# RMSNorm with swish on one Trainium2 core: the last two units of eight rows are swished separately instead of together

## The chip, the cores and the metric

The kernel runs on one core of a Trainium2 chip. The metric is device time in microseconds (us), as the median of several runs. A profile of one execution comes with each kernel: its span is the stretch that the hardware profiler covers, and the execution's own time is somewhat longer than the span.

Four engines work on the data of this kernel or wait for it: VectorE (DVE in the profile), ScalarE (ACT), GpSimd (POOL) and SyncE (SP, which issues all transfers). TensorE (PE) computes nothing here; its queue is used to merge waits.

## The reference

The input x has 16 x 1024 rows of 512 float32 values, gamma has 512 values. Each row is divided by its root mean square, scaled by gamma, and swished (the value times its sigmoid):

```python
def reference(x: np.ndarray, gamma: np.ndarray, eps: float) -> np.ndarray:
    rms = np.sqrt(np.mean(x ** 2, axis=-1, keepdims=True) + eps)
    x_norm = x / rms * gamma
    return (x_norm * (1.0 / (1.0 + np.exp(-x_norm)))).astype(np.float32)
```

So 33.55 MB are read from the chip's memory and 33.55 MB are written to it.

## The kernel before

**Tiling.** The 16384 rows are spread over 128 partitions, 128 rows in each. Rows are counted per partition below, so "row 96" is one row of 512 values in each of the 128 partitions. The rows are worked in units of eight (`cn = 8`), so there are 16 units (`K = 16`), number 0 to 15. On chip they lie in one buffer `xb`, a ring of 96 rows, where everything is done in place: the load writes a unit there, VectorE scales it there, ScalarE swishes it there, and the store reads it from there. Rows 96 to 127 take the places of rows 0 to 31.

**Transfers.** They are larger than a unit, and SyncE issues them all, in an order written out by hand (`order`, L33 to L37), through one hardware queue that 16 DMA engines serve. A piece is a first row and a number of rows. The stores are

```python
    stores = [(0, 32), (32, 32), (64, 16), (80, 16), (96, 24), (120, 8)]
```

A store waits, on SyncE, until the counter `s_swish` has reached the number of units that it needs (`ends`, L56; the wait is at L121 and L122). For the store of rows 96 to 119 that is 15 units, for the one of rows 120 to 127 it is 16. Since SyncE works its list in order, a store that waits holds what comes behind it on SyncE. The last loads are issued after the store of rows 0 to 31 has landed, and before the other stores. At the very end SyncE waits for all stores (L170).

**The work on a unit.** ScalarE squares six of its rows and adds them up (`square`, L211 to L221; L215 is the operation), VectorE does the same for the other two (`sums`, L243 to L250). GpSimd adds eps and raises to the power -0.5 (L183, L189). VectorE multiplies each of the eight rows by its factor and by gamma, one instruction for a row (`norm`, L252 to L259; L255 is the operation), and adds 1 to the counter `s_norm` after the last. ScalarE takes that from `s_norm` and swishes the unit in one instruction (`swish`, L223 to L225), and adds to `s_swish`.

**The order on the engines.** ScalarE's loop (L233 to L240) squares the unit two ahead and then swishes the unit at hand; it runs for units 0 to 13. After the loop, units 14 and 15 are left to swish, and there is nothing left to square. They lie side by side in the ring, and L241 swishes them in one instruction of 16 rows, after a wait for both. VectorE's loop (L267 to L279) sums the next unit and scales the unit at hand, for units 0 to 14; L281 scales unit 15. `take` waits for a number on a counter and lowers the counter by it:

```python
    def take(queue, sem, n=1):
        queue.wait_ge(sem, n).then_inc(sem, -n)
```

Of the kernel before, what the change touches and what calls it, by code (L numbers as in the profile page):

```python
# [9 lines left out]
def kernel(  # L10
# [7 lines left out]
    nc = tc.nc  # L18
    P = nc.NUM_PARTITIONS
    AF = mybir.ActivationFunctionType  # L20
# [18 lines left out]
    cn = 8  # L39
# [13 lines left out]
    K = rows_each // cn  # L53
# [37 lines left out]
    s_norm = nc.alloc_semaphore("s_norm")  # L91
    s_swish = nc.alloc_semaphore("s_swish")
# [4 lines left out]
    def take(queue, sem, n=1):  # L97
        queue.wait_ge(sem, n).then_inc(sem, -n)  # L98
# [9 lines left out]
    def buf(piece):  # L108
        a, n = piece
        at = a % ring  # L110
        assert at + n <= ring, piece
        return xb[:, at : at + n, :]
# [40 lines left out]
    for what, a in order[early:]:  # L153
# [4 lines left out]
        elif what == "gamma":  # L158
            need(
                nc.sync.dma_start(  # L160
                    out=gamma4[0:P:32, :], in_=gamma.partition_broadcast(4)
# [19 lines left out]
    for k in range(K):  # L181
        need(
            nc.gpsimd.tensor_scalar(  # L183
                out=aeps[k % 2], in0=ms[min(k, 1)], scalar1=eps_f, scalar2=None, op0=ALU.add,
# [5 lines left out]
                out=rstd[:, k * cn : (k + 1) * cn], in0=aeps[k % 2], in1=neg_half, op=ALU.pow  # L190
# [13 lines left out]
    def row_of(unit, r, n=1):  # L204
        return flat[:, r * D : ring * D - size + (r + n) * D][:, bass.ds(unit, n * D)]
# [14 lines left out]
        done[-1].then_inc(s_acc, 1)  # L220
        return done  # L221

    def swish(rows, n=1):  # L223
        take(nc.scalar, s_norm, n)
        nc.scalar.activation(out=rows, in_=rows, func=AF.Silu).then_inc(s_swish, n)  # L225

    nc.scalar.preload_act_table_set("silu_and_others")  # L227
    take(nc.scalar, s_land)
# [4 lines left out]
    with nc.scalar.Fori(0, (K - 2) * size, size) as i:  # L233
        new, old = unit_of(i + 2 * size), unit_of(i)
        sq_rows = [row_of(new, r) for r in range(cn - own)]
        old_rows = row_of(old, 0, cn)
        addresses(nc.scalar, [old_rows] + sq_rows)
        take(nc.scalar, s_land)
        square(ms[1], junk, sq_rows)
        swish(old_rows)  # L240
    swish(buf(((K - 2) * cn, 2 * cn)), 2)  # L241

    def sums(to, rows):  # L243
        n = len(rows)
# [22 lines left out]
    with nc.vector.Fori(0, (K - 1) * size, size) as i:  # L267
        new, old = unit_of(i + size), unit_of(i)
        rows = [row_of(old, r) for r in range(cn)]
# [10 lines left out]
    k = K - 1  # L280
# [39 lines left out]
```

## Time and profile before

| | |
|---|---|
| median of 3 runs | 161.79 us (161.56 to 162.26) |
| the profiled execution's own time | 161.8 us |
| its span | 160.5 us |
| VectorE busy | 107.6 us (67%) |
| ScalarE busy | 115.5 us (72%) |
| GpSimd busy | 42.9 us (27%) |
| the DMA queue's packets, share of 16 engines' span | 97.7% |
| memory read and written | 67.12 MB, mean 418 GB/s over the span |
| swishes of eight rows (L225), 14 | mean 3605 ns |
| swish of sixteen rows (L225), 1 | 7030 ns |
| VectorE's scaling of one row (L255), 128 | mean 746 ns |

How to read it: a line such as L225 is a line of the kernel's file, and since `swish` is a helper, all swishes have that line. Busy time counts operations on data, not waits or the issuing of transfers. Scalings follow each other in a pipeline, so eight in a row take less than eight times the mean of one. An issue of a transfer stands under SyncE (SPq) and takes little; the transfer itself lands later, and its packets show only in the views of the DMA. In these, a packet is counted whole in the window in which it starts.

### The profile page before, as it was taken

The numbers are of one execution on the slowest core, as the hardware profiler recorded it, in microseconds if no ns is written. First come the engines' busy times: TensorE is split into PE (matmuls) and PEld (weight loads), VectorE is DVE, ScalarE is ACT, GpSimd is POOL, SyncE is SP. The second block draws the span as 40 slices with busy tenths as digits, with TensorE's granted clock in tenths as the row PEclk, the third lists the DMA queues.
The fourth block names the chain that finished last, engine by engine and source line by source line (L and its number), as shares of the span: only waits on it lengthen the run. The fifth ranks groups of instructions, "written<-read, shape, count | busy, mean of one in ns | idle before, by whom it ended". The sixth has DMA issues, their size and how long they took to land. (4 is left out here: it accounts for less than half of the span.)

```text
span 160.5 us, 847 instructions
## 1 busy us (share of the span) xinstructions
DVE 107.6 (67%) x198; ACT 115.5 (72%) x204; POOL 42.9 (27%) x38
## 2 busy tenths in 40 slices
DVE  0043999798988989898909898989899990000000
ACT  3159389999999999999189999999998009700000
POOL 1004506052441606153305160614325000000000
DMA  7999999999999997969999999969979999299997
GB/s 265 445 427 433 433 482 392 441 474 392 427 397 483 523 441 343 523 270 498 408 392 474 391 419 546 490 294 523 474 310 417 474 408 417 114 588 392 392 392 327
DMA packets 2744, 67.12 MB, mean 418 GB/s; under 512 B 308, under 2 KB 308, under 8 KB 312
## 3 DMA queue, kind: packets, MB, share of 16 engines
q1 hardware_dynamic: 2744, 67.12, 97.7%
HBM read 33.56 MB, written 33.55 MB: 418 GB/s over the span
## 5 line engine op out<-in xcount | busy, mean ns | idle before, releaser
L255 DVE SCALAR_TENSOR_TENSOR xb<-xb,rstd,gamma_sb 128x512 f32 (+1 forms) x128 | 86.1, 746 | 0.0
L225 ACT ACTIVATE xb<-xb (+1 forms) x15 | 57.5, 3834 | 9.4 <-ACTq L98 9.4
L215 ACT ACTIVATE junk<-xb 128x512 f32 (+1 forms) x94 | 54.7, 582 | 12.8 <-ACTq L98 12.8
L246 DVE SCALAR_TENSOR_TENSOR junk_v<-xb 128x512 f32 (+1 forms) x34 | 22.1, 689 | 24.8 <-DVEq L98 24.8
L189 POOL TENSOR_TENSOR rstd<-aeps,neg_half 128x8 f32<-128x8 f32 x16 | 31.8, 1985 | 1.3
L183 POOL TENSOR_SCALAR aeps<-ms 128x8 f32<-128x8 f32 x16 | 10.3, 647 | 78.8 <-DVE junk_v L246 78.8
L215 ACT ACTIVATION_READ_ACCUMULATOR junk<-xb 128x1 f32 x94 | 17.8, 189 | 0.0
L246 DVE DVE_READ_ACCUMULATOR junk_v<-xb 128x1 f32 x34 | 2.8, 83 | 0.0
L227 ACT ACT_TABLE_LOAD x1 | 1.3, 1283 | 1.9 <-PEq L62 1.9
L178 POOL MEMSET gamma<- 128x512 f32 x1 | 0.5, 525 | 1.5 <-POOLq L62 1.5
L263 DVE STREAM_SHUFFLE gamma_sb<-gamma 128x512 f32<-128x512 f32 x1 | 0.7, 718 | 0.0
L301 POOL MEMSET const-float32-0.0<- 128x1 f32 x1 | 0.1, 98 | 0.2 <-issue 0.2
L179 POOL MEMSET neg_half<- 128x8 f32 x1 | 0.1, 105 | 0.0
L301 POOL MEMSET const-bfloat16-1.0<- 128x1 bf16 x1 | 0.1, 102 | 0.0
L301 POOL MEMSET const-uint8-127<- 128x1 uint8 x1 | 0.1, 101 | 0.0
L301 POOL MEMSET const-float32-1.0<- 128x1 f32 x1 | 0.1, 98 | 0.0
L263 DVE LOAD_MASK_SELECT gamma_sb<-gamma x1 | 0.0, 13 | 0.0
## 6 DMA issues: line engine op xcount, KB each, us to landing
xb<-in_x_dram SPq DMA_DIRECT2D x4, 4096.0 KB, 29.7
out_dram<-xb SPq DMA_DIRECT2D x2, 4096.0 KB, 31.0
xb<-in_x_dram SPq DMA_DIRECT2D x3, 2048.0 KB, 13.8
out_dram<-xb SPq DMA_DIRECT2D x1, 6144.0 KB, 15.9
xb<-in_x_dram SPq DMA_DIRECT2D x1, 2816.0 KB, 43.0
xb<-in_x_dram SPq DMA_DIRECT2D x1, 2560.0 KB, 25.0
xb<-in_x_dram SPq DMA_DIRECT2D x2, 1024.0 KB, 5.7
out_dram<-xb SPq DMA_DIRECT2D x1, 2048.0 KB, 20.4
```

Of the source, the lines that this page charges most:

```text
L178: nc.gpsimd.memset(gamma4, 0.0).then_inc(s_zero, 1)
L179: nc.gpsimd.memset(neg_half, -0.5).then_inc(s_half, 1)
L183: nc.gpsimd.tensor_scalar(out=aeps[k % 2], in0=ms[min(k, 1)], scalar1=eps_f, scalar2=None, op0=ALU.add,),
L189: nc.gpsimd.tensor_tensor(out=rstd[:, k * cn : (k + 1) * cn], in0=aeps[k % 2], in1=neg_half, op=ALU.pow),
L215: nc.scalar.activation(out=dummies[j], in_=rows[j], func=AF.Square, scale=inv_d**0.5, accum_out=sums[:, j : j + 1],)
L225: nc.scalar.activation(out=rows, in_=rows, func=AF.Silu).then_inc(s_swish, n)
L227: nc.scalar.preload_act_table_set("silu_and_others")
L246: ins = nc.vector.scalar_tensor_tensor(out=junk_v[j], in0=rows[j], scalar=inv_d, in1=rows[j], op0=ALU.mult, op1=ALU.mult, accum_out=to[:, ...
L255: ins = nc.vector.scalar_tensor_tensor(out=rows[j], in0=rows[j], scalar=factors[j], in1=gamma_sb, op0=ALU.mult, op1=ALU.mult,)
L263: need(nc.vector.stream_shuffle(gamma_sb, gamma4, [0] * 32), s_gld, 16).then_inc(s_gamma, 1)
L301: nc = _bacc.Bacc("TRN2", target_bir_lowering=False, num_devices=1)
```

## The change

`swish` loses its parameter for a number of units, and takes one from `s_norm` and adds one to `s_swish`. Where units 14 and 15 were swished by one instruction of 16 rows, a loop issues two instructions of eight rows, each after a wait for its own unit. The loads, the stores, their order and the other engines' instructions are as before.

```diff
@@ -220,9 +220,9 @@
-    def swish(rows, n=1):
-        take(nc.scalar, s_norm, n)
-        nc.scalar.activation(out=rows, in_=rows, func=AF.Silu).then_inc(s_swish, n)
+    def swish(rows):
+        take(nc.scalar, s_norm)
+        nc.scalar.activation(out=rows, in_=rows, func=AF.Silu).then_inc(s_swish, 1)
@@ -238,7 +238,8 @@
         take(nc.scalar, s_land)
         square(ms[1], junk, sq_rows)
         swish(old_rows)
-    swish(buf(((K - 2) * cn, 2 * cn)), 2)
+    for k in range(K - 2, K):
+        swish(buf((k * cn, cn)))
```

Lines behind L241 move down by one in the changed file.

## The prediction

> **What bounds the kernel now.** I read the chain of waits first, because it shows where the last engine instruction ended, then SyncE's own waits, then the 40 slices, and last the DMA share in short windows of the tail, because only those show transfers.
>
> The chain that ended last, in order of time (start, length, what):
>
> ```profile
> 132.49 0.07 issue
> 132.56 7.03 ACT xb L225
> ```
>
> It stops at 132.56 + 7.03 = 139.59 us, although the span is 160.5 us. The chain knows engine instructions only; the 20.9 us after it belong to transfers. SyncE's own waits (line, what ended the wait, total us, times, longest):
>
> ```profile
> SPq L121 <- ACT xb L225: 42.0, 2, 29.7
> SPq L170 <- DMA out_dram<-xb: 20.0, 1, 20.0
> ```
>
> The reader sees a store (L121) held for 29.7 us by a swish (L225), and then SyncE with nothing left but to wait 20.0 us for stores. Which store: the list of issues from 139 us on has exactly two, of 6144 and 2048 KB, which are rows 96 to 119 and 120 to 127; 288 packets, 8.39 MB in all:
>
> ```profile
> q1 hardware_dynamic: 288, 8.39, 88.9%
> ...
> out_dram<-xb SPq DMA_DIRECT2D x1, 6144.0 KB, 15.9
> out_dram<-xb SPq DMA_DIRECT2D x1, 2048.0 KB, 20.4
> ```
>
> Now the engines before that, in order of time (start, length, engine, line), ScalarE and then VectorE:
>
> ```profile
> 120.27 3.60 ACT L225 ACTIVATE xb<-xb  x1
> 132.56 7.03 ACT L225 ACTIVATE xb<-xb 128x8192 f32<-128x8192 f32 x1 [8.69 <-ACTq L98]
> ```
>
> ```profile
> 121.75 10.69 DVE L255 SCALAR_TENSOR_TENSOR xb<-xb,rstd,gamma_sb 128x512 f32 x16
> ```
>
> ScalarE idles 8.69 us while VectorE scales both last units, eight rows each, in one unbroken stretch; the first unit is done halfway, and nothing takes it up. Last, the transfers in short windows (DMA share is the mean over 16 engines, the last column GB/s; a packet is counted whole in the window where it starts, so a short window can show more than 1):
>
> ```profile
> core 0: us, DVE busy (x) ACT busy (x) POOL busy (x), PEclk, DMA share, GB/s
> 100.00:131.00 31.00, 29.30 (x52) 23.87 (x40) 10.72 (x8) 1.00 0.97 421
> 131.00:137.00 6.00, 1.43 (x3) 4.44 (x1) 0.00 (x0) 1.00 1.01 437
> 137.29:137.32 0.03, 0.00 (x0) 0.03 (x1) 0.00 (x0) 1.00 2.54 1092
> 137.32:140.44 3.12, 0.00 (x0) 2.27 (x1) 0.00 (x0) 1.00 0.00 0
> 140.44:140.60 0.16, 0.00 (x0) 0.00 (x0) 0.00 (x0) 1.00 11.70 4915
> 153.20:153.37 0.17, 0.00 (x0) 0.00 (x0) 0.00 (x0) 1.00 10.71 4626
> 155.02:155.20 0.18, 0.00 (x0) 0.00 (x0) 0.00 (x0) 1.00 3.47 1457
> 159.30:159.47 0.17, 0.00 (x0) 0.00 (x0) 0.00 (x0) 1.00 3.62 1542
> 159.47:160.47 1.00, 0.00 (x0) 0.00 (x0) 0.00 (x0) 1.00 0.01 0
> ```
>
> Share times window times 16 is packet time. At 137.29 that is 2.54 x 0.03 x 16 = 1.22 us: one packet, the last of the older stores, so its engine is free at 137.31 + 1.22 = 138.53. At 140.44 it is 30.0 us: all 16 engines start the 6144 KB store, at 1.87 us a packet. Transfers fill the core's DMA engines up to 137 us (421 and 437 GB/s), then nothing starts for 3.12 us, then the last 8.39 MB run. So DMA bounds the kernel, with one hole, and the hole ends by the 16-row swish.
>
> **The change part by part.** The sum is made against the profiled execution: span 160.47, time 161.8, so 1.33 lie outside; 161.8 is 0.01 above the median of 161.79, so I carry the result over as it is.
>
> 1. Swish of unit 14 alone. VectorE ends that unit at 121.75 + 10.69/2 = 127.10. ScalarE starts some 0.12 later (VectorE's end at 132.44 to ScalarE's start at 132.56), at 127.22, and takes 3.60 (the eight-row row above): done at 130.82, not 139.59. This is the value that the store of rows 96 to 119 waits for (15 units). From the swish's end to the first packets took 140.44 - 139.59 = 0.85 in the tail of before, so its packets are ready at about 131.7. No engine is free before about 137.56: the window 136.34 to 137.32 shows a share of 1.24, that is 1.24 x 0.98 x 16 / 1.215 = 16 packets, the last one of each engine, and they end from 137.56 to 138.53. Slack 5.9 us.
>
> 2. Swish of unit 15. VectorE still ends at 132.44; ScalarE, free since 130.82, runs 132.56 to 136.16, and the 2048 KB store is ready at about 137.0. It is wanted only after eight packets per engine of the store ahead, some 14.6 us later. What the split adds on ScalarE, 2 x 3.60 - 7.03 = 0.17, and one more wait and semaphore step, lie in that cover; without it they would cost 0.17 plus about 0.1.
>
> 3. New overlap: from 127.22 to 130.82 ScalarE swishes beside VectorE's scaling. In the loop eight such scalings took 5.39 beside ScalarE's work, here 10.69/2 = 5.35: 0.04 later for unit 15, covered as in 2. A gain of as much is excluded, since VectorE waits for nothing there.
>
> 4. SyncE. No issue is added or moved in order: the wait for 15 units ends near 130.8 in place of 139.6, the 2048 KB store now waits some 5.3 us for unit 15, and only the final wait (L170) is behind it. An issue takes 0.35. POOL's last work ended at 124.7; nothing of it is passed. The loads are long landed, so nothing collides with an earlier store.
>
> 5. The DMA hole. With packets ready at 131.7, each engine goes from its last older packet straight into the new store. What a hand-over costs I take from the hand-over between the last two stores: at 153.20 to 153.37 all engines start their last packet of 10.71 x 0.17 x 16 / 16 = 1.82 us, so they end at 155.02 to 155.19, and in 155.02 to 155.20 all 16 start the next store. Cost 0, to 0.01. The other bound is what a store pays with nothing ahead: 0.85 to start, and 160.47 - 160.09 = 0.38 from the last byte (159.47 + 0.62) to the end, 1.23 together. I take 0: it is the same kind of transition. Below 0 is excluded, an engine's packets follow in order.
>
> 6. The tail itself. Per engine 8 x 1.82 + 8 x 0.616 (3.62 x 0.17 x 16 / 16) = 19.49. Check: 88.9% of the 22 us queried is 19.56, which holds the first packet's 0.05 extra.
>
> The end is set by the last engine, since a store is dealt out to engines in fixed parts: 138.53 + 19.49 + 0.38 = **158.40**, against 160.47: 2.07 less. Time 161.8 - 2.1 = **159.7** (-1.3%). The hole looks like 3.1 us in the windows, but an engine still works 1.22 us after its last start; that is why I don't take 3.1.
>
> Against this stands a statement of the Trainium skill, "DMA: Bandwidth & Descriptors", section "Anatomy of one DMA": each transfer carries a fixed cost of about 2.0 us besides its bytes, most of it the receipt of the last write. If the queue paid that at a hand-over, the estimate would be 2.07 - 2.0, no gain. The row at 155.02 disagrees that a queued store pays it (0.01 us); what the trace shows at the very end is 0.38 us.
>
> **The rivals.**
>
> A, above: 159.7.
>
> B, the engines even out. At the hole the older stores end spread from 137.56 to 138.53; if the last engine stood at the middle, 138.04, the end would be 0.5 earlier: 159.2. For it speaks that the spread is an accident of one execution; against it, that parts are fixed per engine and rates alike.
>
> C, the hand-over costs what a lone store pays (1.23): 160.9; with as much again for the second, 162.2, no change. Against it the row at 155.02; for it only that this store's packets are larger than those ahead, where the row's are smaller. The 2.0 us of the Trainium skill's page would come out in this case too. That the change does not do what it says, the store still issuing after both swishes, would give 161.8; it is counted here, with little, since the store's wait is for 15 units and the changed code counts each swish by itself.
>
> D, slower: the tail loses speed because engines now enter it out of step, where the hole made all 16 start within 0.16 us. It decides against no change when 8.39 MB take over 160.09 - 138.53 = 21.56 us, below 389 GB/s, and against 162.6 (+0.5%) below 375. Out of step, the stretches of 31 and 6 us above ran at 421 and 437. The slice digits do have single slices (4 us) of 270. Two of them in the tail: 8 us move 2.2 MB, the other 6.2 MB at 431 (8.39/19.49) take 14.4, together 22.4 us: 162.7. All at 270, the far bound, 31.1 us: 171.4. Slices of 48 and 64 KB packets counted by their start swing of themselves, so I give it little.
>
> **How the numbers follow.** A 0.80, B 0.09, C 0.07, D 0.04. A measurement of this kernel tells about 0.5% from no change (its runs span 161.56 to 162.26). A's own range: spread of the last engine +-0.3 and the runs' scatter +-0.4, so 159.2 to 160.3. The range 159.0 to 160.6 takes in B and half the way to C's lower price, and leaves out D and C's upper half. Faster by over 0.5% (below 160.98): A, B and part of C, 0.91; within 0.5%: 0.06; slower: 0.03.
>
> **What would show it.** Right: two swish rows of 3.60 at the end, starting near 127.2 and 132.6; the windows from 137 to 141 without a hole, GB/s above 400; the 6144 KB store's time to landing up from 15.9 to about 22.6 (it stands in the queue first), the 2048 KB store's from 20.4 to about 22; SyncE's longest wait at L121 down from 29.7 to about 21; last landing near 158.4. Wrong: a hole left at 137 to 140 (C), packets of the tail longer than 1.82 and 0.616 us (D), or older stores ending at another time than 138.5, by which the end moves one to one.

## The result and the profile after

The changed kernel takes 160.26 us in the median of 9 runs (159.97 to 161.2), the kernel before 161.84 us beside it (161.56 to 162.43). The ratio is 0.990, 95% interval 0.988 to 0.993: about 1.0% faster. The forecast was 159.7 us, 1.3% faster, with a range of 159.0 to 160.6.

The profiled execution has a span of 158.4 us; 158.40 was forecast. Its own time is 160.09 us, so 1.69 us lie outside the span, where the profile of before had 1.33.

The end of the chain of waits of the changed kernel (start, length, what):

```profile
132.41 0.07 issue
132.48 3.62 ACT xb L225
```

The last swish now ends at 136.10 us instead of 139.59. Before that, the timeline of ScalarE and SyncE:

```profile
127.18 3.62 ACT L225 ACTIVATE xb<-xb 128x4096 f32<-128x4096 f32 x1 [3.39 <-ACTq L98]
130.82 5.63 SPq L121 DMA_DIRECT2D out_dram<-xb  x2
132.48 3.62 ACT L225 ACTIVATE xb<-xb 128x4096 f32<-128x4096 f32 x1 [1.68 <-ACTq L98]
```

Unit 14 is swished while VectorE still scales unit 15, and SyncE issues the store of rows 96 to 119 at 130.82, 8.8 us earlier than before. SyncE's own waits and the two last stores (KB, us from issue to landing):

```profile
SPq L121 <- ACT xb L225: 38.3, 3, 21.0
...
SPq L170 <- DMA out_dram<-xb: 21.9, 1, 21.9
```

```profile
out_dram<-xb SPq DMA_DIRECT2D x1, 6144.0 KB, 22.7
...
out_dram<-xb SPq DMA_DIRECT2D x1, 2048.0 KB, 22.2
```

The longest wait for a swish fell from 29.7 to 21.0 us. Both stores take longer from issue to landing than before (22.7 and 22.2 against 15.9 and 20.4), because they stand in the queue first: that is what a store looks like that was issued early enough. The transfers in short windows (DMA share, then GB/s, as in the prediction):

```profile
core 0: us, DVE busy (x) ACT busy (x) POOL busy (x), PEclk, DMA share, GB/s
136.34:137.31 0.97, 0.00 (x0) 0.00 (x0) 0.00 (x0) 1.00 1.25 541
137.56:138.53 0.97, 0.00 (x0) 0.00 (x0) 0.00 (x0) 1.00 1.88 811
137.32:140.44 3.12, 0.00 (x0) 0.00 (x0) 0.00 (x0) 1.00 1.17 504
157.24:157.30 0.06, 0.00 (x0) 0.00 (x0) 0.00 (x0) 1.00 1.92 819
157.30:158.40 1.10, 0.00 (x0) 0.00 (x0) 0.00 (x0) 1.00 0.00 0
```

The first two lines show the hand-over. From 136.34 to 137.31 start 1.25 x 0.97 x 16 / 1.21 = 16 packets of 32 KB, the last older one of each engine, and these end from 137.56 on. From 137.56 to 138.53 start 1.88 x 0.97 x 16 / 1.82 = 16 packets of 48 KB: each engine goes into the new store as its older work ends. The window that moved nothing before, 137.32 to 140.44, now moves 504 GB/s (large packets counted by their start swing about their mean). The last packets, 1.92 x 0.06 x 16 = 1.84 us of work, are three of 16 KB with 0.61 us each; they start just before 157.30 and end at 157.9, so 0.5 us pass from the last byte to the end of the span. The queue's share of the span rose from 97.7% to 99.0%.

### The profile page after: what moved, and what is told of

Its sections match the earlier page's. It is cut to its first block, busy times and chain, and to the rows that moved or that the text cites. A ratio compares the mean times of both kernels' runs of the same rounds, so it can differ in the third digit from the quotient of the medians.

```text
span 158.4 us, 849 instructions
## 1 busy us (share of the span) xinstructions
DVE 107.6 (68%) x198; ACT 115.7 (73%) x205; POOL 42.8 (27%) x38
## 6 DMA issues: line engine op xcount, KB each, us to landing
xb<-in_x_dram SPq DMA_DIRECT2D x4, 4096.0 KB, 29.7
out_dram<-xb SPq DMA_DIRECT2D x1, 6144.0 KB, 22.7
out_dram<-xb SPq DMA_DIRECT2D x1, 2048.0 KB, 22.2
```

## The experiments

Each time is a median; each ratio is to runs of the kernel before in the same series. That kernel stood at 161.84 us in the first series (the first four experiments), at 161.50 in the second and 161.69 in the third.

**The changed kernel again.** No edit.

> The changed kernel once more, on the chip that runs the next three, to compare them with. Ratio to the kernel before as measured first, 0.988 to 0.993; span 158.3 to 158.8 and time some 1.6 us above it, if the 1.69 us outside the span of its first profile (1.33 in the profile of before) are no accident.

Measured: 160.30 us (160.12 to 161.33), ratio 0.991 (0.988 to 0.994). Between span and time lie 1.6 to 1.7 us in its runs and 1.29 to 1.36 in those of the kernel before. So the 0.35 us that the change adds outside the span are no accident of one profile.

**Two swishes, but the store waits for both.** This undoes the early store alone.

```diff
     ends = [-(-(a + n) // cn) for a, n in stores]
+    ends[-2] = ends[-1]
```

> Units 14 and 15 are swished apart, as in the changed kernel, but the store of rows 96 to 119 waits for 16 units instead of 15. Theory (the gain is the early store alone): unit 15 is done at 136.1, packets at 137.0, still ahead of the first free engine at 137.56, so even this store is early enough and the whole gain stays: 160.3, ratio 0.990. That would say that shortening the end of the swishes from 139.6 to 136.1 is enough, and that a store need not go out after unit 14. Rival (the store must be issued as early as 130.8, because what it needs ahead of its packets is more than the 0.85 us seen with an empty queue): part of the hole returns, 160.8 to 161.8.

Measured: 160.23 us, ratio 0.990 (0.988 to 0.993): the whole gain stays, as forecast. So the early release after unit 14 is not needed at all. The two separate swishes end 3.5 us before the one of 16 rows would, because the first runs while VectorE is still scaling, and that suffices. SyncE issues both last stores together in this kernel, after the second swish:

```profile
136.89 0.81 SPq L122 DMA_DIRECT2D out_dram<-xb  x2
```

Its profile fell on an execution of 161.29 us, the longest of its runs, and shows what made it long (short windows):

```profile
137.32:140.44 3.12, 0.00 (x0) 0.00 (x0) 0.00 (x0) 1.00 1.17 504
137.46:137.73 0.27, 0.00 (x0) 0.00 (x0) 0.00 (x0) 1.00 0.01 0
157.00:157.90 0.90, 0.00 (x0) 0.00 (x0) 0.00 (x0) 1.00 0.09 36
157.90:158.59 0.69, 0.00 (x0) 0.00 (x0) 0.00 (x0) 1.00 0.06 24
158.59:158.65 0.06, 0.00 (x0) 0.00 (x0) 0.00 (x0) 1.00 0.64 273
158.65:159.60 0.95, 0.00 (x0) 0.00 (x0) 0.00 (x0) 1.00 0.00 0
```

There is no hole like that of the kernel before. The first engine is free at 137.46 in this trace, and the store's first packets come only 0.27 us later, not ahead of it as expected; that shows nowhere at the end, which goes by the engine that is last. The last packet that starts, 0.64 x 0.06 x 16 = 0.61 us of work, is alone: between 157.90 and 158.59 only one starts (0.06 x 0.69 x 16 = 0.66 us), and it ends when that last one begins. One DMA engine out of 16 runs a whole microsecond behind the others, and the kernel waits for it.

**One swish, the last stores of 16 rows each.** The swish stays as before; the cut between the stores moves instead.

```diff
-    stores = [(0, 32), (32, 32), (64, 16), (80, 16), (96, 24), (120, 8)]
+    stores = [(0, 32), (32, 32), (64, 16), (80, 16), (96, 16), (112, 16)]
...
-    order += [("landed", 112)] + [("store", a) for a in (32, 64, 80, 96, 120)]
+    order += [("landed", 112)] + [("store", a) for a in (32, 64, 80, 96, 112)]
```

> The swish of 16 rows of before stays; instead the last stores are rows 96 to 111, which needs 14 units and can go at 123.9, and rows 112 to 127, which needs both. Theory (DMA engines must have something to do from 137.5 on): the first 16 rows occupy each engine for 9.7 us from 137.6 to 138.5 on, to 147.3, and the second store is ready at 140.4, so no hole: 160.3, ratio 0.990, without any change of the swishes. Rival (the gain needs the swish itself to be done earlier, because ScalarE's chain sets the end): no change, 161.8, ratio 1.0.

Measured: 159.97 us (159.79 to 160.49), ratio 0.988 (0.986 to 0.991). In the timeline of this kernel the swish is where it was before, and the store of rows 96 to 111 goes out at 123.94. The third line below is the window of the hole:

```profile
123.94 16.05 SPq L121 DMA_DIRECT2D out_dram<-xb  x2
```

```profile
132.60 7.03 ACT L225 ACTIVATE xb<-xb 128x8192 f32<-128x8192 f32 x1 [8.69 <-ACTq L98]
```

```profile
137.32:140.44 3.12, 0.00 (x0) 2.31 (x1) 0.00 (x0) 1.00 1.05 452
```

ScalarE ends as late as in the kernel before, the hole is gone (452 GB/s), and the time is that of the changed kernel or a little less. The rival that ScalarE's chain has to end earlier falls. The spans are alike (158.5 to 158.8 us in most runs of both); the 0.3 us between the medians lie outside the span, 1.29 to 1.36 us here.

**Four stores of eight rows at the end.** More hand-overs between stores in the full queue.

```diff
-    stores = [(0, 32), (32, 32), (64, 16), (80, 16), (96, 24), (120, 8)]
+    stores = [(0, 32), (32, 32), (64, 16), (80, 16), (96, 8), (104, 8), (112, 8), (120, 8)]
...
-    order += [("landed", 112)] + [("store", a) for a in (32, 64, 80, 96, 120)]
+    order += [("landed", 112)] + [("store", a) for a in (32, 64, 80, 96, 104, 112, 120)]
```

> The changed kernel with four stores of 8 rows at the end in place of 24 and 8, so two more hand-overs between stores in the queue, and 16 KB packets instead of 48 KB. Theory (a hand-over in a full queue costs nothing): only the packets' own rate, 24 x 0.615 - 8 x 1.82 = 0.2 us, to 160.5. Rival (a hand-over costs the 1.23 us of a lone store): two more make 2.5 us, 162.8, above the kernel before.

Measured: 160.43 us, ratio 0.992 (0.990 to 0.995), 0.13 us above the changed kernel in the same series. Two hand-overs more cost nothing that shows beyond the rate of smaller packets. The fixed cost of about 2.0 us per transfer, which the Trainium skill gives in "DMA: Bandwidth & Descriptors", section "Anatomy of one DMA — SWDGE (gpsimd) path", is not paid between transfers that stand behind each other in this queue. That section is about transfers that GpSimd issues, and these are SyncE's, so the run says nothing against it.

**ScalarE held before the swish of unit 14.** GpSimd does four powers more, and ScalarE waits for the last; the second kernel has six. The lines that allot `late` and `s_late` are not shown.

```diff
+    for j in range(4):
+        ins = need(
+            nc.gpsimd.tensor_tensor(
+                out=late[:, j * cn : (j + 1) * cn], in0=aeps[(K - 1) % 2], in1=neg_half, op=ALU.pow
+            ),
+            s_eps, K,
+        )
+    ins.then_inc(s_late, 1)
...
+    nc.scalar.wait_ge(s_late, 1)
     for k in range(K - 2, K):
```

> The changed kernel, with ScalarE held before the swish of unit 14 until GpSimd, idle by then, has done four more powers of 2.0 us each (on values nobody uses): the swish starts near 132.8 instead of 127.2 and is done near 136.4. Theory (the DMA queue has 5.9 us of cover left): the store's packets are ready at 137.3, just before the first engine is free at 137.56, so nothing is lost: 160.3, ratio 0.990. Rival (ScalarE's chain sets the end): 5.6 us more, 165.9.

> The same with six powers: the swish starts near 136.8 and is done near 140.4, packets ready at 141.3, some 2.8 us after the last engine is free at 138.5. Theory: the hole is back and all engines start together, 141.3 + 0.1 + 19.5 + 0.4 = 161.3 for the span, 162.9 for the time: of 9.6 us of delay 2.6 show. Rival (each us on ScalarE costs one): 169.9.

Measured with four: 159.89 us, ratio 0.990 (0.989 to 0.992), the full gain although the swish starts 5.2 us late. With six: 161.85 us, ratio 1.002 (1.001 to 1.003), the gain gone. The four powers took 7.95 us, as reckoned, but the six only 11.15 us and not 12, so with six the swish of unit 14 started at 135.58 and not at 136.8. ScalarE's timeline with four, and then with six:

```profile
132.41 7.12 ACT L236 ACTIVATE xb<-xb 128x4096 f32<-128x4096 f32 x2 [8.85 <-ACTq L100]
```

```profile
135.58 7.12 ACT L236 ACTIVATE xb<-xb 128x4096 f32<-128x4096 f32 x2 [12.05 <-ACTq L100]
```

With four, the window of the hole is full:

```profile
137.32:140.44 3.12, 0.00 (x0) 2.21 (x1) 0.00 (x0) 1.00 1.17 504
```

With six, unit 14 is done near 139.2 (its half of 7.12 us), and the windows show the hole again:

```profile
137.22:140.04 2.82, 0.00 (x0) 2.82 (x2) 0.00 (x0) 1.00 0.00 0
140.04:140.20 0.16, 0.00 (x0) 0.16 (x1) 0.00 (x0) 1.00 11.57 4915
```

The packets start 0.85 us after the swish and 19.5 + 0.4 us later the span ends: 140.2 + 19.9 = 160.1, which is the span measured. So the prediction's sum holds with the start put in. Of the 3.2 us between the two kernels' swishes only 1.9 show in the spans (158.2 and 160.1), and of the 5.2 us before that, nothing. Delay on ScalarE is free here until the packets are ready later than the last DMA engine is free.

**Two more waits on ScalarE, or on VectorE.** Where does the time outside the span come from? To the kernel with one swish and stores of 16 rows, two waits that are met since long are added at the end of one engine's program. The diff shows ScalarE's; VectorE's are the same two lines with `nc.vector.wait_ge(s_gamma, 1)`.

```diff
     swish(buf(((K - 2) * cn, 2 * cn)), 2)
+    for _ in range(2):
+        nc.scalar.wait_ge(s_two, 1)
```

> All runs of the kernels with two swishes at the end have 1.6 to 1.7 us between span and time, all with one swish of 16 rows 1.2 to 1.35. They differ in one wait and one swish on ScalarE. Here the kernel with one swish and stores of 16 rows (159.97) gets two more waits on ScalarE at its end, on a counter that stands since long. Theory A (ScalarE's program is longer by two instructions, whatever they are): 1.65 outside the span, 160.3, span unchanged at 158.6. Theory B (it is the swish, an instruction on data): 1.3 outside, 160.0. Theory C (chance): anything.

> The same two waits at the end of VectorE's program instead. If the time outside the span goes by the length of ScalarE's program alone: 1.3 outside, 160.0. If by that of any engine: 1.65, 160.3.

Measured: 159.94 us on ScalarE, 159.87 on VectorE; outside the span 1.44 to 1.59 us and 1.55 to 1.63, against 1.29 to 1.36 without the waits. None of the theories fits exactly: waits alone raise it, less than the full 0.35 us, and on VectorE as well as on ScalarE. Nor is it so much for each instruction: the two held kernels above have one wait more on ScalarE than the changed kernel, and four or six powers more on GpSimd, and 1.62 to 1.74 us outside the span, where the changed kernel has 1.62 to 1.73.

**Four DMA engines given more to do, in the changed kernel and in the one before.** Behind the store of rows 0 to 31, 32 KB of each of four partitions are copied once more, to a scratch tensor.

```diff
-    order += [("landed", 64), ("store", 0), ("load", 80)]
+    order += [("landed", 64), ("store", 0), ("few", 0), ("load", 80)]
...
+        elif what == "few":
+            nc.sync.dma_start(
+                out=scratch, in_=xb[0:P:32, 0:16, :].rearrange("p n d -> p (n d)")
+            ).then_inc(s_few, 16)
...
             nc.sync.wait_ge(st[0], 16)
+            nc.sync.wait_ge(s_few, 16)
```

By the last line SyncE also waits for the copy before it issues the three last loads.

> The changed kernel with one more transfer, behind the store of rows 0 to 31: rows 0 to 15 of four partitions once more, to a scratch tensor, four packets of 32 KB if a partition's 32 KB stay one packet, so four of the 16 DMA engines get 1.21 us more work. Theory (the engine that is last sets the end, and no hole absorbs its lag any more): 0.3 to 1.2 us more than the changed kernel, by whether the last engine is among the four: 160.6 to 161.5. Rival (work evens out over the engines): 131 KB at 430 GB/s, 0.3 us, 160.6.

> The same transfer in the kernel before. Theory (the hole of 2.07 us on the last engine absorbs a lag of 1.21): no change, ratio 1.00. Rival (DMA work bounds this kernel as it does the other): 0.3 to 1.2 us more, ratio 1.002 to 1.007.

Measured: 162.60 us in the changed kernel, ratio 1.006 (1.003 to 1.008), and 164.09 in the one before, ratio 1.015 (1.013 to 1.017). That is 2.3 us more than the changed kernel (160.30 in the first series) and 2.4 us more than the kernel before (161.69). Both expectations missed. The lag was some 2.2 us and not 1.21: in the trace the four packets took 2.3 to 3.0 us each (2.0 to 2.9 in the kernel before). And the kernel before became longer too. (That SyncE waits for the copy as well made the three last loads go out some 2 us later, while the load of rows 80 to 95 still kept the queue full.) The end of the first of the two in short windows:

```profile
157.48:157.70 0.22, 0.00 (x0) 0.00 (x0) 0.00 (x0) 1.00 2.27 968
158.27:159.03 0.76, 0.00 (x0) 0.00 (x0) 0.00 (x0) 1.00 0.25 108
159.03:159.64 0.61, 0.00 (x0) 0.00 (x0) 0.00 (x0) 1.00 0.25 107
```

From 158.27 on the share is 0.25: four of 16 engines still work, the other twelve are done. 131 KB of extra work, 0.3 us if the engines shared it, cost 2.2 us of span (160.6 against 158.4), since nothing evens the engines out. That is the theory of the last engine, shown with a larger lag than planned.

In the kernel before, the hole did take up the lag itself: the last engine ended its older work at 140.86 us by the trace, and the next packets started more than 1.7 us after that.

```profile
140.87:142.58 1.71, 0.00 (x0) 0.88 (x1) 0.00 (x0) 1.00 0.00 0
```

The lag reached the end by another way. ScalarE's timeline there, first without the extra transfer and then with it, when it takes up the load of rows 80 to 95; the last line is the swish of 16 rows with the transfer:

```profile
80.66 0.60 ACT L215 ACTIVATE junk<-xb 128x512 f32 x1 [3.81 <-ACTq L98]
```

```profile
82.83 0.60 ACT L222 ACTIVATE junk<-xb 128x512 f32 x1 [6.18 <-ACTq L100]
...
134.72 7.03 ACT L232 ACTIVATE xb<-xb 128x8192 f32<-128x8192 f32 x1 [8.69 <-ACTq L100]
```

That load counts as landed when its last engine is done, 2.17 us later here; the last swish ends 2.16 us later too (141.75 against 139.59), and so does the span (162.6 against 160.5). So in the kernel before the end hung on that landing at 80.6 us, through the 59 us of ScalarE's chain behind it, and a slow DMA engine reached it there.

**Two waits fewer in TensorE's queue,** in the changed kernel and in the one with stores of 16 rows.

```diff
-                nc.tensor.wait_ge(ld[t], 16)
-        nc.tensor.wait_ge(s_eps, 0 if k < 2 else k).then_inc(s_land, 1)
+                last = nc.tensor.wait_ge(ld[t], 16)
+        if k >= 2:
+            last = nc.tensor.wait_ge(s_eps, k)
+        last.then_inc(s_land, 1)
```

> The changed kernel without the two waits of TensorE's queue that ask for a counter of zero at least, for units 0 and 1. If the time outside the span goes by how many instructions the program has on all engines: 1.3 to 1.5 outside in place of 1.67, 160.0. If TensorE's don't count, or the cause is another: 1.67, 160.3. The span stays at 158.5.

> The kernel with one swish and last stores of 16 rows, without the same two waits. 1.3 outside or less, span 158.6: 159.9 or a little under, the shortest so far; if the waits don't matter, as without this edit, 159.97, ratio 0.988.

Measured: 159.99 us, ratio 0.991 (0.988 to 0.994), and 159.49 us (159.44 to 159.58), ratio 0.986 (0.984 to 0.988). Outside the span 1.61 to 1.70 us and 1.29 to 1.38, unchanged by the edit: these two waits of TensorE's queue don't count there. The second is the shortest kernel of the study; of the 0.5 us to the first in the same series, some 0.35 lie outside the span. Whether the two waits gave it anything against the same kernel with them (0.988, 0.986 to 0.991, in another series) can't be told, as the intervals overlap.

## Why the prediction was right

**Steps 1 to 3 (the swishes).** Right to 0.1 us: starts at 127.18 and 132.48 (127.22 and 132.56 forecast), each 3.62 us. VectorE's 16 scalings took 10.69 us, as before, although ScalarE now swishes beside them. The slack of 5.9 us is borne out from both sides: a delay of 5.2 us cost nothing, and one of 8.4 us brought the hole back.

**Step 4 (SyncE).** Right: issue at 130.82, longest wait 21.0.

**Steps 5 and 6 (the hole and the tail).** Right: the hand-over costs nothing, and the end goes by the last engine. Six profiles show this by their packets, those of the kernels with two swishes and these two last stores, but for the one with six powers. In them the last engine ended its older work at 138.29 to 140.88 us, and the last byte of the two stores was out 19.36 to 19.39 us later each time. The sum had 19.49. The 3.1 us of empty windows were worth 2.1, as reckoned. That the span is 158.40 to the last digit is partly luck: the tail took 0.12 us less than the sum had, and the stretch from the last byte to the end 0.5 us and not 0.38. (That stretch is 0.36 to 0.40 us in eight of the 14 profiles and 0.50 to 0.51 in the other six; why is not known.) The spans of the nine runs go from 158.3 to 159.5 us.

**What was mis-sized** is the 1.33 us outside the span, carried over from the profile of before. They became 1.69, which took back 0.36 us of the 2.07. Step 2 had put the additional wait and swish under the cover of the stores; inside the span they are, but the time outside it grew with them. That is why the profiled execution is at 160.09 and not at 159.7. The other 0.17 us to the median come from the runs' scatter: this execution was among the shorter ones, and runs of 161.0 to 161.3 us have spans of 159.4 to 159.6.

**The rivals.** Rival B, that the engines even out, is out: in the profile after, the engines ended their older work over 0.96 us and their last packets over 0.97 us, and a lag of four engines went into the end undiminished. Rival C, a cost of the hand-over, is out by the windows of the profile after and by the four stores. Rival D, a slower tail, is out: with the engines out of step the tail took no longer.

**What the prediction did not see:** the split of the store's wait was not what mattered. Any one of three edits alone filled the hole: the two swishes with the early store, the two swishes with the late one, or the old swish with another cut between the stores. The cause of the gain is that a store is ready before the last DMA engine runs dry.

**What stays open:** what sets the time outside the span. Going from one swish at the end to two, with a wait, added 0.35 us, and two waits on ScalarE or VectorE some 0.2. One more wait on ScalarE with powers on GpSimd, two more stores on SyncE, and two fewer waits in TensorE's queue changed nothing.

## What to carry to other kernels

When the transfers' queue is full but for one hole, look for what makes a transfer ready before the queue runs dry, and look at the cut between the transfers first: moving it cost no instruction here and gave a little more than splitting the work. Reckon the gain on the DMA engine that is last, from the end of its last packet and not from its start. Compare the time outside the span too when instructions are added: here it took back a sixth of the gain.

## What the runs showed of the hardware

- The DMA engines keep their lags. Each gets a fixed part of every transfer, so an engine that falls behind (by 1 us in the run of 161.29 us, by 2.2 us through four 32 KB packets on four engines) stays behind until all of them idle: a spread of 0.96 us ahead of the tail was still 0.97 us at its end, while the hole of the kernel before made 0.15 us out of 0.95. Landings and the end go by the last.
- Four packets of 32 KB, each from a single partition, took 2.0 to 3.0 us each and held their engines up by about 2.2 us, where packets of that size in a transfer over all 128 partitions took 1.21 us. Why was not tried.
- The time outside the span that the profiler covers is not fixed: 1.28 to 1.38 us for the kernel before, 1.44 to 1.63 us with two met waits more on ScalarE or VectorE, and 1.6 to 1.7 us with a second swish. It does not grow with every instruction, and by what rule it grows is open.
